# A hybrid decoder trunk: group A's level products by row halves, 16-blocks placed by ScalarE, attention scores in two-bank tiles

## The chip, the cores and the metric

The kernel runs on one core of one Trainium2 chip. The metric is the time of one execution on the device in microseconds; less is better. The time before is the median of three runs. The engines are called as the profile calls them: PE (TensorE's matmuls), PEld (its weight loads), DVE (VectorE), ACT (ScalarE), POOL (GpSimd) and SP (the queue that issues DMAs).

## The reference, cut to what matters

Two layers work on a stream of 1024 tokens by 1024 channels. Each layer has a token mixing part and a gated MLP, both between RMS norms. The mixing part projects the stream once, gives its columns to four groups of four heads, joins their outputs and projects them back. The change touches groups A, B and C.

Groups A (HGRN2, key width 64) and B (GLA, key width 32) are gated linear attention, `chunk_gla`: within a stretch of tokens, `attn[i,j] = sum_d q[i,d] k[j,d] exp(b[i,d] - b[j,d])` for `j <= i`, where `b` is the running sum of the log decays; across stretches a state is carried. Group C is causal softmax attention over blocks of 128 queries:

```
sc = (einsum('bqhd,bkhd->bhqk', qn, k_nope) + einsum('bqhd,bkd->bhqk', qr, k_rope)) * scale
p = softmax(where(mask, sc, -1e30))
o = einsum('bhqk,bkhv->bqhv', p, v)
```

Group D (a gated delta rule) and the MLP are not touched.

## The kernel before, in words

A layer runs: projections and group D (pools `p1`, `h`, `w`), then the **mixing stage** in which groups A, B and C are computed together, then the output projection, then the MLP. The mixing stage is the one that the change is in. It fills two stretches of the profiled execution, about 460 to 690 us in layer 0 and about 1943 to 2168 us in layer 1.

In the mixing stage `mixing` (L1068 ff.) drives two generators by turns, step for step, 32 steps of each (`NN`): `group_c` (attention, four heads of eight query blocks) and `ab` (groups A and B). `ab` runs three tiles of `gla_levels`: group B (HP = 4 heads of 32 rows on the 128 partitions), then the two halves of group A (HP = 2 heads of 64 rows), each with seven levels. While the levels of a tile run, `gla_chunks` of the tile before it runs too, one 128-token chunk per step; after the last tile its chunks run alone. A scheduler of the framework fixes the order of each engine's instructions ahead of time, with the program's order as priority and with the tiles' buffers as limits; at run time every engine takes its instructions in that order.

**A level** (`gla_levels`, L440 ff.) with half-block size s = 64, 32, 16, 8, 4, 2, 1 covers, in every block of 2s tokens, the pairs with the query in the second half and the key in the first. DVE (L479), POOL (L480) and ACT (L481) make the decay factors E, POOL multiplies k into them (L483). The queries are spread by head: for group B, DVE makes `qm` (L490) and ACT masks it into `Qb` once per head (L497, the mask column `hm` as the scale). For group A, DVE makes `Qb` directly with one masked product per head, two of 128x512 per level (L499); a head's columns of `Qb` are zero outside its 64 rows. Then PE multiplies 128x128 of K with 128 columns of `Qb` per chunk of 128 tokens (L504), both heads of group A side by side, four chunks to a PSUM tile of one bank; two such tiles make a level of group A, four make one of group B. Every fp32 matmul stands in the trace as two records. The wanted blocks of each tile are then placed in the SBUF tile `at`, which was cleared to zero: for s >= 32 by ACT copies (L509), one for each block row, below that by one DVE copy under a mask for each tile (L511).

**A chunk** (`gla_chunks`, L534 ff.) takes three PSUM tiles: `po` (state product, then the products with `at`, then DVE's sum at L555), `pk` (a transpose that ACT copies, L560) and `pS` (the state's update, which DVE folds in head by head, L565).

**A row of attention blocks** (`scores`, L750 ff.): query block t has (t+1)*128 keys. For each 512 of them one PSUM tile of one bank takes the score product (and on the last the causal mask, a bf16 product); DVE takes its maximum (L764), and for t >= 4 joins the two maxima while it scales (L767, else L769); ACT writes the exponentials of each tile with their sum (L773, an ACTIVATE and a read of its accumulator each); for t >= 4 DVE adds the two sums (L776); DVE takes the reciprocal (L778). `apply` then transposes the weights and multiplies them with the values; it is called two rows later (`LA = 2`).

**PSUM** has eight banks, in this stage split by `PS2 = dict(cs=4, ct=2, pm=2)`: four one-bank score tiles, two for `ct` (attention's other products) and two for `pm`, which all levels and chunks of groups A and B use by turns.

Of the kernel before, what the change touches and what calls it, by code (L numbers as in the profile page):

```python
# [13 lines left out]
ALU = mybir.AluOpType  # L14
# [114 lines left out]
class Body:  # L129
# [310 lines left out]
    def gla_levels(self, HP, load, sc, values, T):  # L440
# [12 lines left out]
        at = [self.t("g", "at", NAT, [128, cpa, HP, 128]) for _ in range(HP)]  # L453
# [5 lines left out]
        for s in LEVELS:  # L459
# [27 lines left out]
            if HP == 4:  # L487
                qm = small([128, 512], "qm", 2)
                qv = qm.rearrange("p (n s) -> p n s", s=s)
                nc.vector.tensor_tensor(out=qv, in0=hf(q, 1), in1=hf(E, 1), op=ALU.mult)  # L490
            for g in range(8 // CB):
                if g * CB % cps == 0:
                    z = slice(g * CB // cps * n2, (g * CB // cps + 1) * n2)
                    Qb = slot([128, cps, HP, 64])
                    for h in range(HP):
                        if HP == 4:
                            nc.scalar.activation(out=Qb[:, :, h, :], in_=qv[:, z], func=AF.Copy, scale=hm[:, h:h + 1])  # L497
                        else:
                            nc.vector.scalar_tensor_tensor(out=Qb[:, :, h, :], in0=hf(q, 1)[:, z], scalar=hm[:, h:h + 1],  # L499
                                                           in1=hf(E, 1)[:, z], op0=ALU.mult, op1=ALU.mult)  # L500
                p = self.ps([128, CB, HP, 64])
                for c in range(CB):
                    cc = g * CB + c
                    self.mm(p[:, c], K[:, cc * 128:(cc + 1) * 128], Qb[:, cc % cps].rearrange("p h i -> p (h i)"))  # L504
                A = at[g * CB // cpa][:, (g * CB) % cpa:(g * CB) % cpa + CB]
                if s >= 32:
                    for n in range(nbc):
                        r = slice(2 * s * n, 2 * s * n + s)
                        nc.scalar.copy(out=A[r, :, :, 2 * s * n + s:2 * s * n + 2 * s], in_=p[r, :, :, n * s:n * s + s])  # L509
                else:  # L510
                    nc.vector.copy_predicated(  # L511
                        out=A.rearrange("p c h (n e s) -> p (c h) n e s", e=2, s=s)[:, :, :, 1, :],
                        mask=mk.rearrange("p (n s) -> p n s", s=s)[:, None, :, :].to_broadcast([128, CB * HP, nbc, s]),
                        data=p.rearrange("p c h (n s) -> p (c h) n s", s=s))
# [19 lines left out]
    def gla_chunks(self, HP, T, out, f0):  # L534
# [9 lines left out]
        for c in range(8):  # L544
# [5 lines left out]
            for h in range(HP):  # L550
                self.mm(po[:, h * 64:h * 64 + 64], T["at"][c // (8 // HP)][:, c % (8 // HP), h, :], vc[:, h * 64:h * 64 + 64],
# [157 lines left out]
    def group_c(self, l, ckv, wv, load, krd, out):  # L709
# [40 lines left out]
        def scores(h, t):  # L750
# [3 lines left out]
            ps = []  # L754
            nm = small([128, 2], "nm", 4)
            for a in range(0, nk, 512):
                e = min(nk, a + 512)
                dg = e == nk
                p = self.ps([128, 512], "cs")[:, 0:e - a]
                self.mm(p, qc, K[:, a:e], True, not dg)  # L760
                if dg:
                    self.mm(p[:, e - a - 128:e - a], id16, caus, False, True)
                i = len(ps)
                nc.vector.tensor_reduce(out=nm[:, i:i + 1], in_=p, axis=AX.X, op=ALU.max)  # L764
                ps.append(p)
            if len(ps) == 2:
                nc.vector.tensor_scalar(out=nm[:, 0:1], in0=nm[:, 0:1], scalar1=nm[:, 1:2], scalar2=-scale, op0=ALU.max, op1=ALU.mult)  # L767
            else:
                nc.vector.tensor_scalar(out=nm[:, 0:1], in0=nm[:, 0:1], scalar1=-scale, scalar2=None, op0=ALU.mult)  # L769
            P = small(None, "P", LA + 1)  # L770
            sm = small([128, 2], "sm", 4)
# [898 lines left out]
```

## Time and profile before

| | us |
|---|---|
| runs before | 2966.41, 2962.98, 2966.25 |
| median | 2966.25 |
| the profiled execution's own time | 2966.38 |
| its span, first to last instruction | 2964.6 |
| busy in it: PE | 2743.4 (93%) |
| busy in it: DVE | 1881.0 (63%) |
| busy in it: ACT | 1272.3 (43%) |
| busy in it: POOL | 1192.4 (40%) |

The shares are means over stages with different limits. Matmuls are pipelined and their modelled ends overlap, so a PE that shows as busy need not be at its peak. A row of a group of instructions gives its count, the union of its busy time, the mean duration of one in ns, and the idle time of the engine ahead of them with what ended it.

### The profile page before, as it was taken

To read this page: it belongs to the slowest core of one execution; us is meant where nothing else is said; L and a number is where in the kernel's file an instruction comes from. 1 tells how busy PE (TensorE), PEld (TensorE's weight loads), DVE (VectorE), ACT (ScalarE), POOL (GpSimd) and SP (SyncE) were. 2 spreads that over 40 slices of the span, in tenths; PEclk is the share of its full clock that TensorE was granted. 3 is DMA by queue.
4 is the path that set the end of the run, shared out by engine and by line. 5 is a ranking of instruction groups with operands and counts; after the bars stand their busy time and mean duration, and the time that the engine had idled before them with its cause. 6 is when DMAs were issued, how large, how long until landed. Compare 5 with 4: busy or idle time off the path is not lost. (4 is left out here: it accounts for less than half of the span.)

```text
span 2964.6 us, 40009 instructions
## 1 busy us (share of the span) xinstructions
PE 2743.4 (93%) x14928; PEld 2223.9 (75%) x14928; DVE 1881.0 (63%) x2740; ACT 1272.3 (43%) x2338; POOL 1192.4 (40%) x1008
## 2 busy tenths in 40 slices
PE   7999898899869999999979998988998699999998
PEld 6787695677758888888767876856777588888887
DVE  5564426883697777764645645268836977777645
ACT  4523337555443333354434233375554433333443
POOL 2122654445765444300231327544457644443001
PEclk9999899999989999999989999999999899999999
DMA  3222653114423322376522226431143232223765
GB/s 122 70 83 69 238 185 122 60 45 135 136 68 100 100 98 99 121 261 187 174 70 69 84 76 236 178 122 62 43 135 135 68 103 96 99 100 103 258 197 192
DMA packets 152307, 362.94 MB, mean 122 GB/s; under 512 B 24337, under 2 KB 35889, under 8 KB 152113
## 3 DMA queue, kind: packets, MB, share of 16 engines
q1 hardware_dynamic: 152112, 360.39, 36.7%
q8 instruction: 117, 1.92, 0.3%
q14 instruction: 78, 0.63, 0.1%
HBM read 259.08 MB, written 101.25 MB: 122 GB/s over the span
## 5 line engine op out<-in xcount | busy, mean ns | idle before, releaser
L209 PE MATMUL pd<-h,wr 128*128 128x512 f32 x2624 | 664.8, 404 | 14.9 <-ACT wr L197 8.9
L198 POOL TENSOR_TENSOR wr<-wst,wr 128x512 fp32r<-128x512 f32 (+1 forms) x176 | 336.1, 1912 | 772.7 <-ACT wr L197 771.4
L209 PEld LDWEIGHTS pd<-h,wr 128*128 128x128 f32 x2624 | 493.9, 191 | 134.9 <-issue 11.4
L197 ACT CAST wr<-wst 128x512 fp32r<-128x512 f32 (+1 forms) x260 | 196.9, 759 | 373.0 <-PE pd L209 251.4
L209 PE MATMUL pd<-wr,h 128*128 128x256 f32 x1920 | 248.1, 290 | 1.1 <-issue 1.1
L209 PE MATMUL pm<-h,wr 128*128 128x512 f32 x848 | 235.2, 401 | 11.8 <-DVE x L1375 11.7
L209 PEld LDWEIGHTS pd<-wr,h 128*128 128x128 f32 x1920 | 240.8, 198 | 2.8 <-issue 1.4
L198 DVE TENSOR_TENSOR h<-st,h 128x1024 fp32r<-128x1024 f32 x120 | 152.6, 1273 | 122.6 <-ACT h L197 119.8
L209 PEld LDWEIGHTS pm<-h,wr 128*128 128x128 f32 x848 | 162.0, 191 | 52.2 <-DVE x L1375 12.5
L209 PE MATMUL pd<-wr,f 128*128 128x512 f32 x768 | 186.1, 399 | 11.4 <-POOL wr L198 10.5
L197 ACT CAST h<-st 128x1024 fp32r<-128x1024 f32 x120 | 125.6, 1048 | 146.4 <-PE pd L209 82.8
L209 PE MATMUL pd<-h 128*128 128x512 f32 x816 | 185.6, 389 | 0.0
L209 PEld LDWEIGHTS pd<-wr,f 128*128 128x128 f32 x768 | 143.6, 189 | 45.4 <-POOL wr L198 12.2
L209 PEld LDWEIGHTS pd<-h 128*128 128x128 f32 x816 | 153.2, 188 | 31.8
L209 PE MATMUL pm<-h 128*128 128x512 f32 x720 | 165.6, 390 | 0.8 <-DVE h L198 0.8
L1311 DVE SCALAR_TENSOR_TENSOR g<-z,pp,g 128x512 f32<-128x512 f32 x176 | 152.7, 868 | 7.3
L209 PEld LDWEIGHTS pm<-h 128*128 128x128 f32 x720 | 134.8, 188 | 29.6 <-DVE h L198 1.6
L1434 POOL TENSOR_TENSOR y<-y,gb 128x512 f32<-128x512 f32 x24 | 38.6, 1616 | 272.9 <-ACT fc L230 137.0
L215 PE MATMUL pm<-g,g 128*128 128x128 f32 (+1 forms) x672 | 118.3, 323 | 30.0 <-issue 12.9
L215 PEld LDWEIGHTS pm<-g,g 128*128 128x128 f32 x672 | 96.9, 198 | 57.4 <-issue 29.9
L1379 ACT COPY x<-pm 128x512 f32<-128x512 f32 x120 | 70.2, 585 | 152.8 <-PE pm L209 152.8
L209 PE MATMUL pm<-hs,wr 128*128 128x512 f32 x528 | 130.0, 394 | 3.2 <-POOL wr L198 3.2
(366 smaller groups left out, 5465.8 us busy)
## 6 DMA issues: line engine op xcount, KB each, us to landing
st<-gd SPq DMA_DIRECT2D x144, 256.0 KB, 3.0
wst<-in_wgu_dram SPq DMA_DIRECT2D x44, 512.0 KB, 3.6
ust<-in_wgu_dram SPq DMA_DIRECT2D x44, 512.0 KB, 3.6
gd<-g SPq DMA_DIRECT2D x88, 256.0 KB, 2.0
d<-in_wdn_dram SPq DMA_DIRECT2D x40, 512.0 KB, 5.5
td<-d SPq DMA_DIRECT2D x40, 512.0 KB, 3.1
st<-td SPq DMA_DIRECT2D x80, 256.0 KB, 3.6
st<-in_wdn_dram SPq DMA_DIRECT2D x68, 256.0 KB, 3.8
```

What stands on the lines that cost most here:

```text
L197: self.marks["hi"] = self.nc.scalar.copy(out=hi, in_=src)
L198: (eng or self.nc.gpsimd).tensor_tensor(out=lo, in0=src, in1=hi.bitcast(F32), op=ALU.subtract)
L209: mm = lambda x, y, **k: self.nc.tensor.matmul(out, lhsT=x, rhs=y, skip_group_check=onto, **k)
L215: self.nc.tensor.matmul(out, lhsT=lhsT, rhs=rhs, start=start, stop=stop)
L1311: nc.vector.scalar_tensor_tensor(out=c, in0=x[:, j:j + 512], scalar=w(j), in1=c, op0=ALU.mult, op1=ALU.add)
L1379: nc.scalar.copy(out=x, in_=p)
L1434: (dve if last and n else pool).tensor_tensor(out=y[t][:, c], in0=y[t][:, c], in1=g_post[:, c], op=ALU.mult)
```

## The change

It has three parts.

1. **Group A's level products by row halves.** For HP = 2 the masked queries `Qb` go. One DVE product per level makes `qm` from all 128 rows, with the constant scale `qscale` in place of the mask column. PE multiplies, per chunk and head, the head's 64 rows of K (64 rows by 128 columns as weights) with the head's 64 rows and 64 columns of `qm`: 16 matmuls of 64x64 operands in place of 8 of 128x128. Each head has a PSUM tile of its own (one bank) for all eight chunks, so both are filled side by side, and the placing follows after all 16. `at` is kept per head, [128, 8, 128]. Group B keeps its products.
2. **16-blocks are placed by ScalarE.** The limit between ACT's copies and DVE's masked copy moves from s >= 32 to s >= 16, for groups A and B: at s = 16 each tile is placed by four ACT copies of 16 partitions x 128 elements.
3. **A row of attention shares a two-bank tile.** The score tile becomes [128, 1024] in place of [128, 512], two of them in place of four (`cs=2`). All score products of a row go into it; then come one maximum over all keys, one scaling, one ACTIVATE with one read of the accumulator, one reciprocal. The join of the maxima and the sum of the two sums go.

```diff
@@ -450,7 +450,9 @@
         q, k, b = (load(j, slot()) for j in range(3))
         W = HP * 64
         CB, cpa, cps = 512 // W, 8 // HP, 1024 // W
-        at = [self.t("g", "at", NAT, [128, cpa, HP, 128]) for _ in range(HP)]
+
+        two = HP == 2
+        at = [self.t("g", "at", NAT, [128, 8, 128] if two else [128, cpa, HP, 128]) for _ in range(HP)]
         for x in at:
             nc.gpsimd.memset(x, 0.0)
         Qst, Kst = slot(), slot()
@@ -484,34 +486,46 @@
             mk = self.cm[:, LEVELS.index(s) * 64:(LEVELS.index(s) + 1) * 64]
             nbc = 64 // s
             n2 = cps * 64 // s
-            if HP == 4:
-                qm = small([128, 512], "qm", 2)
-                qv = qm.rearrange("p (n s) -> p n s", s=s)
+            qm = small([128, 512], "qm", 2)
+            qv = qm.rearrange("p (n s) -> p n s", s=s)
+            if two:
+                nc.vector.scalar_tensor_tensor(out=qv, in0=hf(q, 1), scalar=qscale, in1=hf(E, 1), op0=ALU.mult, op1=ALU.mult)
+            else:
                 nc.vector.tensor_tensor(out=qv, in0=hf(q, 1), in1=hf(E, 1), op=ALU.mult)
-            for g in range(8 // CB):
-                if g * CB % cps == 0:
-                    z = slice(g * CB // cps * n2, (g * CB // cps + 1) * n2)
-                    Qb = slot([128, cps, HP, 64])
-                    for h in range(HP):
-                        if HP == 4:
-                            nc.scalar.activation(out=Qb[:, :, h, :], in_=qv[:, z], func=AF.Copy, scale=hm[:, h:h + 1])
-                        else:
-                            nc.vector.scalar_tensor_tensor(out=Qb[:, :, h, :], in0=hf(q, 1)[:, z], scalar=hm[:, h:h + 1],
-                                                           in1=hf(E, 1)[:, z], op0=ALU.mult, op1=ALU.mult)
-                p = self.ps([128, CB, HP, 64])
-                for c in range(CB):
-                    cc = g * CB + c
-                    self.mm(p[:, c], K[:, cc * 128:(cc + 1) * 128], Qb[:, cc % cps].rearrange("p h i -> p (h i)"))
-                A = at[g * CB // cpa][:, (g * CB) % cpa:(g * CB) % cpa + CB]
-                if s >= 32:
+
+            def place(A, p):
+
+                if s >= 16:
                     for n in range(nbc):
                         r = slice(2 * s * n, 2 * s * n + s)
-                        nc.scalar.copy(out=A[r, :, :, 2 * s * n + s:2 * s * n + 2 * s], in_=p[r, :, :, n * s:n * s + s])
+                        nc.scalar.copy(out=A[r, :, 2 * s * n + s:2 * s * n + 2 * s], in_=p[r, :, n * s:n * s + s])
                 else:
                     nc.vector.copy_predicated(
-                        out=A.rearrange("p c h (n e s) -> p (c h) n e s", e=2, s=s)[:, :, :, 1, :],
-                        mask=mk.rearrange("p (n s) -> p n s", s=s)[:, None, :, :].to_broadcast([128, CB * HP, nbc, s]),
-                        data=p.rearrange("p c h (n s) -> p (c h) n s", s=s))
+                        out=A.rearrange("p c (n e s) -> p c n e s", e=2, s=s)[:, :, :, 1, :],
+                        mask=mk.rearrange("p (n s) -> p n s", s=s)[:, None, :, :].to_broadcast([128, 8, nbc, s]),
+                        data=p.rearrange("p c (n s) -> p c n s", s=s))
+
+            if two:
+                ps = [self.ps([128, 8, 64]) for _ in range(2)]
+                for c in range(8):
+                    for h in range(2):
+                        r = slice(64 * h, 64 * h + 64)
+                        self.mm(ps[h][:, c, :], K[r, c * 128:(c + 1) * 128], qm[r, c * 64:(c + 1) * 64])
+                for h in range(2):
+                    place(at[h], ps[h])
+            else:
+                for g in range(8 // CB):
+                    if g * CB % cps == 0:
+                        z = slice(g * CB // cps * n2, (g * CB // cps + 1) * n2)
+                        Qb = slot([128, cps, HP, 64])
+                        for h in range(HP):
+                            nc.scalar.activation(out=Qb[:, :, h, :], in_=qv[:, z], func=AF.Copy, scale=hm[:, h:h + 1])
+                    p = self.ps([128, CB, HP, 64])
+                    for c in range(CB):
+                        cc = g * CB + c
+                        self.mm(p[:, c], K[:, cc * 128:(cc + 1) * 128], Qb[:, cc % cps].rearrange("p h i -> p (h i)"))
+                    A = at[g * CB // cpa][:, (g * CB) % cpa:(g * CB) % cpa + CB]
+                    place(A.rearrange("p c h t -> p (c h) t"), p.rearrange("p c h t -> p (c h) t"))
             if s == 64:
 
                 bc = [128, 8, 64]
@@ -548,7 +562,8 @@
             if c:
                 self.mm(po, T["Q"][:, cl], St, True, False)
             for h in range(HP):
-                self.mm(po[:, h * 64:h * 64 + 64], T["at"][c // (8 // HP)][:, c % (8 // HP), h, :], vc[:, h * 64:h * 64 + 64],
+                a = T["at"][h][:, c, :] if HP == 2 else T["at"][c // 2][:, c % 2, h, :]
+                self.mm(po[:, h * 64:h * 64 + 64], a, vc[:, h * 64:h * 64 + 64],
                         c == 0, c == 0 or h == HP - 1)
             dv = small([128, W], "dv", 2)
             nc.gpsimd.tensor_tensor(out=hv(dv), in0=hv(vc), in1=T["dots"][:, c, :, None].to_broadcast([128, HP, 64]), op=ALU.mult)
@@ -751,31 +766,22 @@
             Q, K = QK[h]
             nk = (t + 1) * 128
             qc = Q[:, t * 128:(t + 1) * 128]
-            ps = []
-            nm = small([128, 2], "nm", 4)
+
+            p = self.ps([128, 1024], "cs")
+            nm = small([128, 1], "nm", 4)
             for a in range(0, nk, 512):
                 e = min(nk, a + 512)
                 dg = e == nk
-                p = self.ps([128, 512], "cs")[:, 0:e - a]
-                self.mm(p, qc, K[:, a:e], True, not dg)
+                self.mm(p[:, a:e], qc, K[:, a:e], True, not dg)
                 if dg:
-                    self.mm(p[:, e - a - 128:e - a], id16, caus, False, True)
-                i = len(ps)
-                nc.vector.tensor_reduce(out=nm[:, i:i + 1], in_=p, axis=AX.X, op=ALU.max)
-                ps.append(p)
-            if len(ps) == 2:
-                nc.vector.tensor_scalar(out=nm[:, 0:1], in0=nm[:, 0:1], scalar1=nm[:, 1:2], scalar2=-scale, op0=ALU.max, op1=ALU.mult)
-            else:
-                nc.vector.tensor_scalar(out=nm[:, 0:1], in0=nm[:, 0:1], scalar1=-scale, scalar2=None, op0=ALU.mult)
+                    self.mm(p[:, e - 128:e], id16, caus, False, True)
+            nc.vector.tensor_reduce(out=nm, in_=p[:, 0:nk], axis=AX.X, op=ALU.max)
+            nc.vector.tensor_scalar(out=nm, in0=nm, scalar1=-scale, scalar2=None, op0=ALU.mult)
             P = small(None, "P", LA + 1)
-            sm = small([128, 2], "sm", 4)
-            for i, p in enumerate(ps):
-                nc.scalar.activation(out=P[:, i * 512:i * 512 + p.shape[1]], in_=p, func=AF.Exp, scale=scale, bias=nm[:, 0:1],
-                                     accum_out=sm[:, i:i + 1])
-            if len(ps) == 2:
-                nc.vector.tensor_tensor(out=sm[:, 0:1], in0=sm[:, 0:1], in1=sm[:, 1:2], op=ALU.add)
+            sm = small([128, 1], "sm", 4)
+            nc.scalar.activation(out=P[:, 0:nk], in_=p[:, 0:nk], func=AF.Exp, scale=scale, bias=nm, accum_out=sm)
             rc = small([128, 1], "rc", 4)
-            nc.vector.reciprocal(out=rc, in_=sm[:, 0:1])
+            nc.vector.reciprocal(out=rc, in_=sm)
             return P, rc
 
         def apply(h, t, P, rc):
@@ -1638,7 +1644,7 @@
 NP, NU, NUL, NFIN = 10, 4, 4, 6
 
 LA = 2
-PS2 = dict(cs=4, ct=2, pm=2)
+PS2 = dict(cs=2, ct=2, pm=2)
 NN = (32, 32)
 
 HALF = (slice(0, 2), slice(2, 4))
```

## Rows read from the trace of the kernel before

**Rows 1.** Busy time by stretch, layer 0's mixing stage; columns in the first line.

```profile
core 0: us, PE busy (x) PEld busy (x) DVE busy (x) ACT busy (x) POOL busy (x), PEclk, DMA share, GB/s
460.00:680.00 220.00, 197.66 (x1187) 150.90 (x1185) 183.32 (x385) 130.79 (x337) 90.85 (x82) 0.97 0.18 59
...
480.00:520.00 40.00, 31.36 (x156) 23.25 (x157) 29.75 (x56) 34.02 (x86) 19.65 (x15) 1.00 0.20 60
500.00:560.00 60.00, 49.68 (x269) 34.89 (x267) 55.19 (x104) 39.06 (x101) 24.93 (x21) 1.00 0.21 66
580.00:640.00 60.00, 56.51 (x371) 45.75 (x369) 55.39 (x118) 31.89 (x81) 30.50 (x26) 0.94 0.21 65
```

**Rows 2.** Chain that ended last, layer 1's mixing stage (1943 to 2168 us), shares by line.

```profile
by line: PE pm L215 23.1%; PE ct L215 13.5%; PE cs L215 8.5%; DVE g L499 7.2%; DVE at L511 5.9%; issue 5.3%; PE ct L219 5.1%; ACT g L497 3.2%; DMA K<-kr 2.5%; DVE S L565 2.4%; DVE nm L764 1.9%; ACT g L481 1.9%; DVE qm L490 1.7%; DMA g<-Av 1
```

**Rows 3.** Groups by shape, 455 to 690 us: count, busy us, mean ns, idle before.

```profile
L511 DVE COPY_PREDICATED at<-cm,pm 128x512 f32<-128x512 int32 x40 | 37.1, 955 | 5.6 <-PE pm L215 5.0
L499 DVE SCALAR_TENSOR_TENSOR g<-g,cf,g 128x512 f32<-128x512 f32 x28 | 32.1, 1165 | 1.4 <-ACT g L481 1.4
...
L773 ACT ACTIVATE P<-cs,nm 128x512 f32<-128x512 f32 x24 | 16.5, 687 | 4.4 <-DVE nm L767 3.8 <-DVE nm L769 0.5
L764 DVE TENSOR_REDUCE nm<-cs 128x1 f32<-128x512 f32 x24 | 16.3, 681 | 1.3 <-PE cs L215 1.2
...
L773 ACT ACTIVATION_READ_ACCUMULATOR P<-cs,nm 128x1 f32 x48 | 9.6, 200 | 0.0
...
L509 ACT COPY at<-pm 32x256 f32<-32x256 f32 x16 | 5.8, 362 | 5.6 <-PE pm L215 5.4
L776 DVE TENSOR_TENSOR sm<-sm 128x1 f32<-128x1 f32 x16 | 5.7, 358 | 2.0 <-ACT P L773 1.9
...
L560 ACT COPY kT<-pm 128x128 f32<-128x128 f32 x21 | 5.5, 263 | 11.3 <-PE pm L219 11.2
...
L773 ACT ACTIVATE P<-cs,nm 128x128 f32<-128x128 f32 x8 | 2.9, 363 | 3.6 <-DVE nm L769 3.6
...
L764 DVE TENSOR_REDUCE nm<-cs 128x1 f32<-128x128 f32 x8 | 2.3, 286 | 1.2 <-PE cs L215 1.1
```

**Rows 4.** The same groups, ACT alone.

```profile
L529 ACT COPY dots<-pm 128x16 f32<-128x16 f32 x2 | 0.3, 172 | 4.6 <-PE pm L215 4.6
```

**Rows 5.** Timeline: a level of group A's first half; start us, us, engine.

```profile
592.14 1.78 DVE L499 SCALAR_TENSOR_TENSOR g<-g,cf,g 128x512 f32<-128x512 f32 x2
...
594.38 1.95 PE L215 MATMUL pm<-g,g 128*128 128x128 f32 x16
...
595.32 0.68 DVE L764 TENSOR_REDUCE nm<-cs 128x1 f32<-128x512 f32 x1
...
595.92 2.43 DVE L511 COPY_PREDICATED at<-cm,pm 128x512 f32<-128x512 int32 x2
```

**Rows 6.** Timeline of PE: levels of group A's second half.

```profile
637.99 1.06 PE L215 MATMUL pm<-g,g 128*128 128x128 f32 x8
...
639.10 1.06 PE L215 MATMUL pm<-g,g 128*128 128x128 f32 x8
639.99 0.41 PE L215 MATMUL pm<-S,g 128*128 128x128 f32 x2
...
643.20 1.06 PE L215 MATMUL pm<-g,g 128*128 128x128 f32 x8
```

**Rows 7.** Timeline of PE in group D: 64-row products (64*128) and their neighbours.

```profile
208.10 0.71 PE L215 MATMUL pm<-vn,kl 128*128 128x128 f32 x4
208.75 1.71 PE L215 MATMUL pm<-d,d 64*128 64x128 f32 x16
...
138.30 0.72 PE L215 MATMUL pm<-d,d 64*128 64x128 f32 x8
```

**Rows 8.** Busy time by stretch around a fall of the clock, columns as in rows 1.

```profile
555.00:561.00 6.00, 4.86 (x38) 4.32 (x39) 5.92 (x14) 2.15 (x8) 3.66 (x4) 1.00 0.01 3
562.00:568.00 6.00, 6.00 (x23) 5.25 (x24) 2.44 (x8) 2.02 (x4) 2.51 (x3) 0.50 0.00 1
```

## The prediction

> **What bounds the kernel now.** I read the stretches first, then the chain, then the groups, then timelines of single levels. All three edits lie in the mixing stage, about 225 us in each of two layers, 450 of 2966 us; the reader needs no other stage. In layer 0's 220 us PE shows 197.7 us busy and DVE 183.3, ACT 130.8 [rows 1]. No engine is full all the time. DVE is full from 500 to 560 us (55.2 of 60) and from 580 to 640 (55.4 of 60), but in the second of these PE shows 56.5 of 60 as well. Between 480 and 520 us, where group B's levels run, it is ACT that is nearly full: 34.0 of 40. The chain of layer 1's stage says the same [rows 2]: PE's `pm`, `ct` and `cs` lines hold 23.1 + 13.5 + 8.5 + 5.1 = 50%, DVE's named lines 7.2 + 5.9 + 2.4 + 1.9 + 1.7 = 19%. So DVE's work is worth its chain share at most, and PE stands close behind. I take both layers as alike.
>
> **Part 1, the masked products.** Two DVE products of 1.165 us per level become one: 14 of 28 go in a layer, 16.3 us of DVE work [rows 3]. Their line holds 7.2% of 225 us of chain = 16.2 us [rows 2], so half of them is worth **-8.1 us** a layer.
>
> PE: a level's product is 16 records in 1.95 us now [rows 5], and 8 take 1.06 [rows 6]: (1.06 - 0.275) / 7 = 0.112 us apart, the last one's tail being some 0.275 (an estimate from 16 records: 1.95 - 15 x 0.112). After the change it is 32 records of 64 rows. Group D already has such records: 8 of them took 0.72 us [rows 7]. One after another they would take 7 x 0.112 + 0.275 = 1.06; in four pairs 3 x 0.112 + 0.275 = 0.61. So upper and lower halves run side by side, and 32 records need about the 16 places of before. What is left over, 0.72 - 0.61 = 0.11 us, is a slow first record. Entering this mode shows too: four full-height records from 208.10 leave room for the next at 208.55, and the 64-row ones begin at 208.75 [rows 7], 0.1 us beyond one spacing. Leaving it I take as equal. That is 0.3 us more per level, 14 levels, 4.2 us; half of it on the chain, as PE holds half: **+2.1 us**. Bounds per level: no gain below 0.1, and 1.8 if nothing overlaps.
>
> Placing: until now a level's first tile was placed while PE filled the second. Now both heads' tiles fill together, so the first placing starts about one half product later, 1.06 us [rows 6], and both `pm` banks are held meanwhile. Behind them queue the chunk's `po`, then `pk` and `pS`, and DVE's update. In group A's first half DVE is late anyway: at 594.38 PE started, its first half was done by about 595.4, but DVE was at a maximum (595.32, 0.68 us) and placed from about 595.9 on [rows 5]. There I count nothing. In the second half's last five levels, about 5.2 us from one (637.99) to the next (643.20) with the chunk's products 0.9 us behind the second half product's start [rows 6], the wait is open: 5 x 0.95 = **+4.8 us** (the half run less the 0.1 by which it is usually late). Bounds: 0 to 14 x 1.06 = 14.8.
>
> **Part 2, the 16-blocks.** One of five masked levels leaves DVE: 8 of 40 copies of 0.955 us, 7.6 us of work [rows 3]; of the chain's 5.9% = 13.3 us a fifth, **-2.7 us**. ACT gets 32 copies of 16 partitions x 128 elements, which no row shows. The nearest are 128 elements at 0.263 us and, on the two sides, 256 elements at 0.362 [rows 3] and 16 elements at 0.172 [rows 4]. I take 0.263, the same element count: 8.4 us a layer, 5.5 to 11.6. Half of it falls on group B, where ACT is 85% busy [rows 1], and displaces masked queries and exponentials; I count a quarter of that half, **+1.0 us**. Group A's half lies beside free ACT time (31.9 of 60 busy from 580 to 640); with that cover gone it would cost up to 4.2.
>
> **Part 3, attention.** Sixteen rows a layer have t >= 4. A maximum costs 0.154 us plus 1.03 ns an element (0.681 at 512, 0.286 at 128), an exponential 0.255 plus 0.84 ns (0.687 and 0.363), a read of the sum 0.200 [rows 3]. Joining two tiles saves one fixed part each, and the 0.358 us addition: DVE 16 x (0.154 + 0.358) = 8.2 us, ACT 16 x (0.255 + 0.200) = 7.3 us. DVE's lines hold a fifth of the chain, so **-1.6 us**; ACT's I put against part 2's copies. Against it: two score tiles in place of four, so row t's products wait for the exponentials of row t - 2. Thirty-two rows in 225 us come 7 us apart, and the maximum starts only after all products, a bank's product later; the two-row lead covers both. Cost 0; if the cover goes, about 1 us in each of 16 rows.
>
> **The sum** per layer: -8.1 + 2.1 + 4.8 - 2.7 + 1.0 - 1.6 = -4.5, for both -9.0. The profiled execution took 2966.38 us (span 2964.6), 0.1 above the median, so the forecast is **2957 us**; its own range is 2945 to 2960.
>
> **The rivals.** *More gain*: DVE is the bound throughout its full stretches. 16.3 + 7.6 + 8.2 = 32.1 us of work leave DVE in each layer; 120 of the 220 us are full, 17.5 us, less 4 of PE's cost, for two layers 27: 2939. For it: just before the clock fell to 0.50 (the 1.2 GHz level) at 562, DVE was busy 5.9 of 6 us and PE 4.9 [rows 8]; six us at half clock cost three, and a fuller PE could spare them. Against it: PE at 56.5 of 60. Chance 0.12.
>
> *No change*: PE takes the place as soon as DVE is lighter, what DVE gave goes back in changes of mode and later placings: 2966. For it: half the chain is PE's. Chance 0.24.
>
> *Slower by the pair of banks*: each level must have both `pm` banks at once and gives neither back before its last product. Then all 28 levels pay 1.06 us, 29.7 in all, plus 4.2 for PE, against the relief of 8.1 + 2.7 - 1.0 + 1.6 = 11.4 a layer, 22.8: +11, **2977**. It decides from (22.8 - 4.2) / 1.06 = 18 levels of 28 on. For it: the levels of rows 6 take the two banks one after the other, 1.1 us apart, each as it comes free. Against it: late DVE hides it in the first half, and DVE will be less late at the updates too. Chance 0.17.
>
> *Slower by the halves in turn*: 32 records a level one after another, 1.5 us a level over my 0.3, 42 us of PE, half on the chain: 2978. Against it stand the 0.72 us of rows 7; for it the other row there, 16 records in 1.71 us, not far below the 15 x 0.112 + 0.275 = 1.96 of one after another. The order chosen ahead of time could come out so here. Chance 0.07.
>
> The Trainium skill (TensorE: Matmul & The Clock Gate, LDWEIGHTS (loading the stationary operand)) has a rule that leads there: a load costs by its columns, whatever its rows, so twice as many loads would take twice the time, and by that alone the sum is this rival's 2978. The same page (Part 3) lets loads of different row groups overlap; the 0.72 us of rows 7 agree with that, and the sum stays at the forecast.
>
> **How the numbers follow.** The forecast has 0.40, the rivals 0.12, 0.24, 0.17, 0.07. About 0.2%, 6 us, is what a measurement can tell. Faster: 0.40 + 0.12 = 0.52; the same 0.24; slower 0.17 + 0.07 = 0.24. The range reaches to the larger gain and beyond both slower cases, as the placing's bound alone spans 30 us: 2930 to 2980.
>
> **What would show it.** The masked product line at 14 a layer instead of 28; group A's products as 64-row records, a level's 32 within 2.1 us (3.6 would show the last rival); 16-partition copies near 0.26 us; maxima and exponentials of 640 to 1024 elements at 0.154 us + 1.03 ns and 0.255 us + 0.84 ns an element; DVE near 151 of 220 us; the stage shorter by 4 to 5 us in each layer. A longer wait of PE or ACT for `pm` in all levels of group A would show the pair of banks; a stage unchanged with DVE lighter, PE as the bound. Wrong altogether would be a difference outside the two mixing stages, or an ACT that holds group B back by more than the 4 us its copies take.

## The result and the profile after

The changed kernel takes **3063.2 us** (median of 4 runs, 3052.2 to 3079.6), the kernel before 2966.3 beside it: ratio **1.0327 [1.0301, 1.0352]**, 97 us slower. Forecast were 2957 us and at most 2980. The profiled execution took 3079.6 us, the longest of the four. The page, busy time and granted clock (each digit a fortieth of the span, in tenths):

```profile
span 3077.9 us, 40827 instructions
...
PE 2863.1 (93%) x15376; PEld 2324.7 (76%) x15376; DVE 1829.4 (59%) x2632; ACT 1281.7 (42%) x2338; POOL 1189.8 (39%) x1008
...
PEclk9999899679989999999989999996899899999999
```

DVE has 108 instructions and 52 us less, where 64 us of work were meant to go. PE is busy 120 us more. The clock is low in the slices of the two mixing stages and hardly elsewhere. From the last product of L209 ahead of a stage to the first one behind it, layer 0 takes 297.8 us in place of 242.1 and layer 1 293.3 in place of 241.6: 107 of the 113 us by which the span grew. In layer 0's stage PE is busy for 270.8 us (214.5 before) and idle for 27.0 (27.6): all that was added is busy PE. By stretches of layer 0 (columns as in [rows 1]):

```profile
core 0: us, PE busy (x) PEld busy (x) DVE busy (x) ACT busy (x) POOL busy (x), PEclk, DMA share, GB/s
460.00:730.00 270.00, 245.97 (x1337) 190.03 (x1338) 154.89 (x314) 128.79 (x323) 94.80 (x85) 0.82 0.16 54
480.00:520.00 40.00, 31.95 (x138) 24.06 (x136) 21.23 (x38) 35.65 (x90) 17.04 (x12) 0.87 0.13 38
560.00:580.00 20.00, 20.00 (x89) 15.06 (x89) 9.35 (x17) 8.16 (x22) 6.54 (x7) 0.67 0.01 2
580.00:600.00 20.00, 20.00 (x79) 16.88 (x79) 5.52 (x13) 3.01 (x7) 6.38 (x6) 0.50 0.08 26
600.00:620.00 20.00, 20.00 (x100) 16.66 (x99) 9.70 (x22) 4.74 (x11) 4.87 (x5) 0.66 0.17 53
620.00:640.00 20.00, 20.00 (x111) 17.46 (x109) 11.52 (x27) 6.13 (x16) 2.28 (x3) 0.74 0.28 93
```

Where DVE was full and the clock at 0.94 [rows 1], PE is now busy without a gap, at a clock of 0.50 to 0.74, and DVE works 5.5 to 11.5 of 20 us. So DVE was relieved and PE became the bound, at half its speed for some of the time. Twice the length times (1 - granted clock) gives the time at half clock (1.2 GHz): 96 us of layer 0's stage and 85 of layer 1's, against 14 and 10 before. The chain of layer 1 says the same; PE's `pm` line holds 38.3% (23.1% in [rows 2]), DVE's placing 2.7% and its masked products 1.4%:

```profile
by line: PE pm L215 38.3%; PE ct L215 18.2%; PE cs L215 9.1%; issue 7.4%; PE ct L219 4.9%; DVE g L481 3.4%; DVE at L503 2.7%; DVE qm L492 1.4%; PE pm L219 1.4%; ACT g L522 1.4%; POOL g L485 1.3%; DVE g L533 1.2%; DVE g L535 1.0%; ACT PT L79
```

The groups that answer to [rows 3], layer 0's stage (line, engine, shapes, count, busy us, mean ns, idle before):

```profile
L215 PE MATMUL pm<-qm,g 64*128 64x64 f32 x448 | 59.6, 324 | 5.9 <-POOL g L478 2.5 <-DVE rc L784 1.9 <-DVE nm L779 1.5
...
L503 DVE COPY_PREDICATED at<-cm,pm 128x512 f32<-128x512 int32 x32 | 31.5, 1013 | 37.9 <-PE pm L215 37.6
...
L492 DVE SCALAR_TENSOR_TENSOR qm<-g,g 128x512 f32<-128x512 f32 x14 | 11.8, 843 | 7.7 <-PE pm L215 6.3 <-ACT g L471 1.3
...
L501 ACT COPY at<-pm 16x128 f32<-16x128 f32 x32 | 8.2, 256 | 8.2 <-PE pm L215 7.8
...
L778 DVE TENSOR_REDUCE nm<-cs 128x1 f32<-128x1024 f32 x3 | 3.7, 1221 | 1.3 <-PE cs L215 1.3
...
L782 ACT ACTIVATE P<-cs,nm 128x1024 f32<-128x1024 f32 x3 | 3.3, 1106 | 0.0
```

Counts are as forecast, 14 products among them, and so are these durations: 16-partition copies of 256 ns (263 were taken), a maximum of 1024 elements in 1.221 us (1.21 by the two terms), an exponential in 1.106 (1.12). A product takes 0.843 us where 1.165 was taken. New is DVE's idle time for PE ahead of the placing: 37.6 us, where [rows 3] has 5.0. Four levels of group A show why:

```profile
start us, us, engine line op out<-in xcount [idle before <-releaser]
545.95 2.00 PE L215 MATMUL pm<-qm,g 64*128 64x64 f32 x32 [0.93 <-POOL g L478]
...
570.05 2.00 PE L215 MATMUL pm<-qm,g 64*128 64x64 f32 x16
...
572.08 1.06 ACT L501 COPY at<-pm 16x128 f32<-16x128 f32 x4 [0.91 <-PE pm L215]
...
573.03 2.00 PE L215 MATMUL pm<-qm,g 64*128 64x64 f32 x16
...
585.88 3.67 PE L215 MATMUL pm<-qm,g 64*128 64x64 f32 x16
...
592.02 3.67 PE L215 MATMUL pm<-qm,g 64*128 64x64 f32 x16
...
694.63 2.94 PE L215 MATMUL pm<-qm,g 64*128 64x64 f32 x32
```

The first level alternates its halves: 32 records in 2.00 us. The level from 570.05 runs head 0's 16 records, 2.00 us by themselves, and head 1's from 573.03. The one from 585.88 does the same at half clock, 3.67 us a half. By the order of PE's instructions, 10 of 14 levels in a layer run six or more products (two records each) of one half before the other half. Seven of them run all eight, then other products, then the other half, as the second and third here: 4.0 us at the full clock. The other three, the last line among them, overlap where the half changes and take 2.94 to 3.17 us. Why the order is so was not measured by itself; it fits that each half's products are given to PE as their own `pm` bank comes free, since the halves alternate in the two kernels below that give both banks at one time.

### The profile page after: what moved, and what is told of

Read it like the earlier page. It is cut to its first block, busy times and chain, and to the rows that moved or that the text cites. A ratio compares the mean times of both kernels' runs of the same rounds, so it can differ in the third digit from the quotient of the medians.

```text
span 3077.9 us, 40827 instructions
## 1 busy us (share of the span) xinstructions
PE 2863.1 (93%) x15376; PEld 2324.7 (76%) x15376; DVE 1829.4 (59%) x2632; ACT 1281.7 (42%) x2338; POOL 1189.8 (39%) x1008
## 5 line engine op out<-in xcount | busy, mean ns | idle before, releaser
L209 PE MATMUL pd<-h,wr 128*128 128x512 f32 x2624 | 666.0, 404 | 15.9 <-ACT wr L197 8.9
L209 PEld LDWEIGHTS pd<-h,wr 128*128 128x128 f32 x2624 | 494.9, 191 | 135.9 <-ACT wr L197 11.6
L209 PE MATMUL pd<-wr,h 128*128 128x256 f32 x1920 | 246.9, 290 | 0.0
L209 PE MATMUL pm<-h,wr 128*128 128x512 f32 x848 | 235.5, 401 | 11.8 <-DVE x L1381 11.8
L209 PEld LDWEIGHTS pd<-wr,h 128*128 128x128 f32 x1920 | 239.8, 197 | 1.8 <-issue 0.4
L209 PEld LDWEIGHTS pm<-h,wr 128*128 128x128 f32 x848 | 162.2, 192 | 51.6 <-DVE x L1381 12.7
L209 PE MATMUL pd<-wr,f 128*128 128x512 f32 x768 | 190.3, 405 | 11.5 <-POOL wr L198 10.0
L209 PE MATMUL pd<-h 128*128 128x512 f32 x816 | 185.6, 389 | 0.0
L209 PEld LDWEIGHTS pd<-wr,f 128*128 128x128 f32 x768 | 146.6, 194 | 46.9 <-POOL wr L198 11.8
L209 PEld LDWEIGHTS pd<-h 128*128 128x128 f32 x816 | 153.2, 188 | 31.8
L209 PE MATMUL pm<-h 128*128 128x512 f32 x720 | 167.1, 393 | 0.0
L209 PEld LDWEIGHTS pm<-h 128*128 128x128 f32 x720 | 136.6, 190 | 28.5
L215 PEld LDWEIGHTS pm<-qm,g 64*128 64x128 f32 x896 | 110.0, 230 | 31.1 <-issue 16.9
L209 PE MATMUL pm<-hs,wr 128*128 128x512 f32 x528 | 130.6, 395 | 2.6 <-POOL wr L198 2.6
L209 PE MATMUL pd<-hs,wr 128*128 128x512 f32 x528 | 129.2, 393 | 0.0
```

The lines of the kernel that those rows point to most:

```text
L209: mm = lambda x, y, **k: self.nc.tensor.matmul(out, lhsT=x, rhs=y, skip_group_check=onto, **k)
L215: self.nc.tensor.matmul(out, lhsT=lhsT, rhs=rhs, start=start, stop=stop)
```

## Experiments

Each run is also told as a share of the 2966 us by its ratio. full and pm4 were timed once and have no interval. Stretches of layer 0's mixing stage stand in the table, as worked out from the timeline: *B* from the stage's start to DVE's first sum of a chunk of group B (group B's levels), *A1* from there to the first sum of group A's first half (its levels beside B's chunks), *A2* to the first sum of its second half, *rest* the last chunks and what is left of attention, and us at half clock in the whole stage, from its granted clock. Each row is of one execution: in bench (below), whose stages are those of the kernel before, instruction for instruction, the two stages have 3 and 17 us at half clock where the kernel before has 14 and 10, so ten us in that column say little.

| kernel | median us | ratio [95%] | B | A1 | A2 | rest | half clock |
|---|---|---|---|---|---|---|---|
| before | 2966 to 2970 | 1 | 95.8 | 67.5 | 45.0 | 33.8 | 14 |
| changed | 3063.2 | 1.0327 [1.0301, 1.0352] | 100.3 | 95.6 | 63.2 | 38.6 | 96 |
| p1 | 3049.0 | 1.0259 [1.0229, 1.0289] | 99.3 | 82.4 | 54.6 | 40.7 | 61 |
| p23 | 2995.4 | 1.0080 [1.0065, 1.0096] | 101.1 | 66.6 | 51.1 | 36.5 | 27 |
| full | 3039.4 | timed once | 100.1 | 73.1 | 65.4 | 39.5 | 44 |
| pm4 | 3032.1 | timed once | 108.6 | 61.7 | 59.4 | 45.2 | 61 |
| wide | 3023.9 | 1.0183 [1.0168, 1.0199] | 105.8 | 72.1 | 52.8 | 38.6 | 34 |
| paircs | 3023.0 | 1.0176 [1.0163, 1.0189] | 90.2 | 80.1 | 57.3 | 38.9 | 61 |
| p2 | 2987.6 | 1.0054 [1.0041, 1.0068] | 98.3 | 63.6 | 46.8 | 38.3 | 10 |
| p3 | 2986.7 | 1.0054 [1.0042, 1.0066] | 96.5 | 66.8 | 52.7 | 35.3 | 21 |
| p2a | 2992.3 | 1.0078 [1.0063, 1.0094] | 97.7 | 64.4 | 50.1 | 41.4 | 27 |
| p3b | 3008.8 | 1.0132 [1.0114, 1.0149] | 98.8 | 70.6 | 50.0 | 40.7 | 27 |
| act0 | 2969.3 | 1.0001 [0.9989, 1.0013] | 95.9 | 60.1 | 44.5 | 42.4 | 21 |
| act0_n34 | 2963.1 | 0.9987 [0.9976, 0.9997] | 96.2 | 60.1 | 47.3 | 36.3 | 12 |

**Which part costs.** p1 is the changed kernel with parts 2 and 3 taken back, p23 with part 1 taken back.

> Part 1 alone, the row halves; parts 2 and 3 as in the kernel before. Common to every theory that puts the loss on part 1: 3050 to 3090 us, the clock at half for over 70 us in each mixing stage. If the loss were due to the two-bank score tiles or to ACT's placing: 2955 to 2975, since the halves alone would then be the small gain that was forecast.

> Parts 2 and 3 alone, group A's queries masked on DVE as before, full-height products. If part 1 is the whole loss: 2945 to 2970 us, by the forecast's own terms (2 x (-2.7 + 1.0 - 1.6) = -6.6) near 2960, and no more than about 15 us at half clock in a mixing stage, as before. If the pair of score banks or the 16-row copies carry a part of the loss: above 2980.

p1 is 77 us slower, p23 24: together 101, beside 97 for all three parts. Part 1 has most of the loss, a little less than expected (3049 us for 3050 or more, 61 and 58 us at half clock for over 70). Of the 35 us by which layer 0's stage grew, 25 are in the levels of group A. p23 came out by its second case: parts 2 and 3 lose by themselves where the forecast had 6.6 us of gain.

**Height, columns, order.** Four kernels take part 1 apart. full undoes only the height:

```diff
-  r = slice(64 * h, 64 * h + 64)
-  self.mm(ps[h][:, c, :], K[r, c * 128:(c + 1) * 128], qm[r, c * 64:(c + 1) * 64])
+  self.mm(ps[h][:, c, :], K[:, c * 128:(c + 1) * 128], qh[h][:, c * 64:(c + 1) * 64])
```

> The changed kernel, its records of group A's level products made of full height again: queries masked per head on DVE, all 128 rows of K as weights, and the same 16 products of 64 columns into the same two pm banks. So the number of records, the banks and the waits for them stay as changed; only the height differs. Theory clock (half-height records let the granted clock fall): the half-clock time falls from some 90 us a mixing stage to under 30, and although 32 records now run one after another (3.6 us a level) and DVE has its 14 products back, the time is under 3030 us, near 3000. Theory turn (the loss is the records one after another, 1.5 us a level, and the low clock only follows from DVE waiting for PE): 3050 us or more, the clock at half as long as in the changed kernel.

Between the two: 3039.4, the clock at half for 44 and 34 us. Against p23, with the same work on DVE, 32 records of 64 columns in place of 16 of 128 cost 44 us; 28 levels by 1.65 (3.6 - 1.95 [rows 5]) are 46. That is near, but not the same thing by itself: full has 24 us more at half clock than p23, worth up to 12, and takes its banks otherwise. Against the changed kernel it is 24 us *faster* although DVE has 14 products a layer more to do, with 79 us at half clock in the two stages in place of 181.

pm4 sets `PS2 = dict(cs=1, ct=2, pm=4)`; paircs takes a level's two halves as one tile:

```diff
-  ps = [self.ps([128, 8, 64]) for _ in range(2)]
+  pp = self.ps([128, 2, 8, 64], "cs")
+  ps = [pp[:, h] for h in range(2)]
```

> The changed kernel with four pm banks in place of two, paid for by one two-bank score tile in place of two. The order chosen ahead then has the two halves alternating in nearly every level. Theory turn: a level of group A takes 2.0 to 2.2 us of PE at full clock instead of 3.6, the clock stays as before (under 20 us at half in a stage), 2960 to 2990 us. Theory clock: the halves run side by side but are half-height records all the same, the clock is at half for over 60 us in a stage, 3020 us or more. Its one score tile could cost by itself up to 1 us in each of 64 rows of attention blocks, 64 us in all, which would show as DVE and PE idle in attention at full clock.

> The changed kernel, a level's two halves in one tile of two banks, which it takes from the score tiles: one wait for both banks, so the order chosen ahead alternates the halves. The pm banks are left to group B and the chunks. Theory turn (pairs side by side take a level back to 2.0 to 2.2 us of PE, the clock follows): under 50 us at half clock in a stage, 2980 to 3020 us with the cost of parts 2 and 3 still in it. Theory height: still over 70 us at half clock, 3040 us or more. Attention and the levels now share two tiles, which could cost by itself up to 1 us in each of 28 levels.

In both the halves alternate, and a level takes what was forecast at full clock; two levels of paircs in the timeline (start us, us):

```profile
548.37 3.68 PE L215 MATMUL cs<-qm,g 64*128 64x64 f32 x32 [0.26 <-POOL g L478]
...
579.84 2.00 PE L215 MATMUL cs<-qm,g 64*128 64x64 f32 x32
```

That takes back 31 and 40 us, but not the rest: the clock is at half for some 60 us a stage, where theory turn had under 20 and under 50. pm4 came out close to theory clock (over 60 us, 3020 or more); paircs fits neither of its theories. pm4, with one score tile, also has 8 us more in B than the changed kernel and 7 more in the rest. At half clock the same 32 records take 3.68 us. The trace shows what stands ahead of the longest fall in paircs:

```profile
543.60:547.60 4.00, 3.20 (x24) 2.69 (x23) 3.42 (x8) 3.11 (x6) 0.86 (x2) 1.00 0.00 0
547.60:578.30 30.70, 27.46 (x154) 22.54 (x153) 19.44 (x28) 11.60 (x31) 19.84 (x14) 0.50 0.06 18
```

The clock falls at 547.6 us, ahead of the stage's first half-height record (548.37) and behind a stretch with gaps in PE, so these records did not start that fall. Of the seven falls in the changed kernel's layer 0, two come behind 4 us in which PE had no gap (at 576.1, the longest, and 627.3), the other five behind 4 us in which it was busy for 1.1 to 3.6. What starts a fall, and why the clock falls as often in pm4 and paircs, is not shown.

wide keeps the half height and moves 128 columns:

```diff
-  self.mm(ps[h][:, c, :], K[r, c * 128:(c + 1) * 128], qm[r, c * 64:(c + 1) * 64])
+  e = min(c * 64 + 128, 512)
+  self.mm(ps[h].rearrange("p c i -> p (c i)")[:, c * 64:e], K[r, c * 128:(c + 1) * 128], qm[r, c * 64:e])
```

> The changed kernel, where each half-height record of group A's level products moves 128 columns in place of 64: its own 64 and the next chunk's, which the next product of the same head overwrites (the last chunk of a head keeps 64). Order, banks, weights, waits and results stay; only the columns that PE moves per record double. In turn, records are 0.112 us apart with 64 columns or 128, so at full clock the products take no longer. Theory columns (the clock falls because records of 64 columns in turn leave PE without columns to move for half of its busy time): more columns make the kernel faster, half-clock time from some 90 us a mixing stage to under 50, 3005 to 3045 us. Theory height (rows that stand idle let the clock fall): the clock is at half as long as in the changed kernel, 3055 us or more.

Nearly twice the columns, and 39 us faster, with 34 and 38 us at half clock. That speaks for theory columns, but the order moved too: only 4 levels of a layer, not 10, run six or more products of one half in turn. So bench measures the disputed thing by itself:

```diff
+  up, lo, al = slice(0, 64), slice(64, 128), slice(0, 128)
+  one = lambda p, r, c, n: self.mm(p[:, 0:n], K[r, c * 128:c * 128 + 128], q[r, c * 64:c * 64 + n])
+  turn = lambda ru, rl, n: [(p, r, c, n) for p, r in ((a, ru), (b, rl)) for c in range(8)]
+  for seq in (turn(al, al, 64), turn(up, lo, 64), [x for c in range(8) for x in ((a, up, c, 64), (b, lo, c, 64))],
+              turn(up, lo, 128), turn(al, al, 128)):
+      for _ in range(16):
+          for x in seq: one(*x)
+      apart()
```

> The kernel before with streams of products behind its end, on PE alone with nothing to wait for, from two loaded tiles; their results are dropped. Five blocks of 512 records, between blocks 96 records of full height and 512 columns (some 40 us): (1) full height, 64 columns, 16 records into one bank, then 16 into the other; (2) the same with the upper half's 16 and then the lower half's 16; (3) halves alternating, 64 columns; (4) as (2) with 128 columns; (5) as (1) with 128 columns. Theory columns: (1) and (2) alike fall to half clock and take some 110 us each, (3) to (5) stay at full clock with some 30, 57 and 57 us. Theory height: (1) and (5) at full clock, (2) and (4) at half. Theory gaps (the clock falls only where PE waits, so not in a stream without waits): all five at full clock, 57, 57, 30, 57, 57 us.

Stretches of bench inside block (1), the products between, (2), those between, (3), (4) and (5):

```profile
core 0: us, PE busy (x) PEld busy (x) DVE busy (x) ACT busy (x) POOL busy (x), PEclk, DMA share, GB/s
3020.00:3070.00 50.00, 50.00 (x450) 50.00 (x449) 0.00 (x0) 0.00 (x0) 0.00 (x0) 1.00 0.00 1
3072.00:3112.00 40.00, 40.00 (x94) 17.67 (x93) 0.00 (x0) 0.00 (x0) 0.00 (x0) 1.00 0.00 0
3120.00:3190.00 70.00, 70.00 (x430) 70.00 (x430) 0.00 (x0) 0.00 (x0) 0.00 (x0) 0.50 0.00 1
3200.00:3236.00 36.00, 36.00 (x85) 15.96 (x84) 0.00 (x0) 0.00 (x0) 0.00 (x0) 1.00 0.00 0
3238.00:3266.00 28.00, 28.00 (x508) 28.00 (x504) 0.00 (x0) 0.00 (x0) 0.00 (x0) 1.00 0.01 2
3310.00:3354.00 44.00, 44.00 (x487) 44.00 (x487) 0.00 (x0) 0.00 (x0) 0.00 (x0) 1.00 0.01 1
3398.00:3452.00 54.00, 54.00 (x486) 54.00 (x485) 0.00 (x0) 0.00 (x0) 0.00 (x0) 1.00 0.00 1
```

From their first to their last record the blocks take 57.0, **81.7**, 28.5, 46.6 and 57.1 us. All three theories miss. Full height with 64 columns keeps the clock, half height with 128 columns too, and so do half-height pairs; only half height *and* 64 columns *in turn* runs at half clock, with PE busy for 70.00 of 70 us and waiting for nothing. The products behind it have the full clock again. Each block ran once, in this one order. That is the form which part 1 gave to 10 levels of 14, and the stretch at 580 us above shows it in the kernel, among other products; the three levels that overlap in part ran at the full clock. Within one half the records of blocks (2) and (4) come 0.213 and 0.112 us apart, but at each change of the half some of them overlap. So block (4) takes less than (5), and (2) less than twice (1).

**Why parts 2 and 3 lose.** p2 and p3 are each part alone; p3b takes two-bank tiles but leaves maxima, exponentials and sums apart; p2a leaves group B's 16-blocks with DVE.

```diff
 p3b:  + pp = self.ps([128, 1024], "cs")
       - p = self.ps([128, 512], "cs")[:, 0:e - a]
       + p = pp[:, a:e]
 p2a:  - if s >= 16:
       + if s >= (16 if HP == 2 else 32):
```

> Part 3 alone: a row's scores in one two-bank tile, two of them in place of four single banks. Theory banks (a row waits for the exponential of the second row before it, so attention cannot run between group B's levels): 2980 to 2995, and a stretch of some 20 us in group B's levels without score products. Theory ACT: 2955 to 2968.

> The kernel before with a row's score banks taken as one tile of two banks, two such tiles in place of four single banks; maxima, exponentials and sums stay apart, one for each bank. So it is part 3's wait without its savings on DVE and ACT. Theory banks (the wait costs what part 3 costs): 2985 to 3000, the 17 us of part 3 alone and up to 8 us a stage for the savings that are missing. Theory joined (the long maximum and exponential of 1024 elements delay DVE and ACT): 2966 to 2975.

Theory banks holds: two tiles without the joining (p3b) cost 39 us, more than its range of 2985 to 3000 had, joining them gives back 23, and part 3 is left with 16. The place was wrong: it is A2 that grows, by 7.7 us in p3, not group B's levels. The weights of the score products, p3 and then before: idle time ahead of them for an exponential grew from 1.7 to 6.1 us in layer 0. These 4.4 us are part of the 9.2 by which p3's stage is longer there; in p3b that wait is 4.8 us, and the stage 18 us longer. The rest was not traced to a wait.

```profile
L215 PEld LDWEIGHTS cs<-K,Q 128*128 128x128 f32 x96 | 15.2, 194 | 10.0 <-ACT P L784 6.1 <-DVE Q L764 2.2 <-issue 1.4
```

```profile
L215 PEld LDWEIGHTS cs<-K,Q 128*128 128x128 f32 x96 | 15.0, 194 | 5.3 <-issue 1.8 <-ACT P L773 1.7 <-DVE Q L747 1.2
```

> Part 2 alone: ACT places the 16-blocks, the rest as before. Theory ACT (parts 2 and 3 together cost 27 us because ACT's 32 copies a layer of group B's half lie on a full ACT and hold its levels back): 2980 to 2995. Theory banks (the pair of score banks costs them): 2955 to 2968.

> Part 2 alone, for group A's levels alone; group B's 16-blocks stay with DVE. Theory B (ACT's copies cost in group B's levels, where ACT is nearly full): the 18 us of part 2 alone are gone, 2960 to 2970. Theory order (the cost lies in the two stretches behind and at the stage's end, where rows of attention are left over): 2978 or more.

p2 is 16 us slower, and p2a, without group B's half, 23: theory B falls. The table's layer 0 shows the smaller part of p2's loss: that stage is 4.9 us longer, layer 1's 12.3, with 34 us at half clock there (10 before). In p2, p2a and act0 (below) three rows of attention are left behind the last chunk, two before, and in p2a's A2 the clock falls beside the small sums of q times k (2 columns a record, 213 ns apart at half clock). Four runs tried these. `n34` merges the streams with `NN = (34, 32)`, `dw` moves 64 columns of the same constants in those sums:

> Part 2 alone (ACT places the 16-blocks of both groups) with the weight of 34 to 32. Theory leftover (most of part 2's 18 us is the same three rows at the end of the stage, 14 and 17 us in place of 10): 2965 to 2975. Theory ACT (its copies hold the levels back): 2980 or more, as without the weight.

> The control: the kernel before with the same weight of 34 to 32. One and a half rows are left behind its last chunk, so there is less to win. Theory leftover: 0 to 6 us faster a stage, 2955 to 2966. Theory moved: 2964 to 2972.

> ACT's placing of group A's 16-blocks alone, with the same 64 columns in place of 2 or 4. Its trace shows those 16 records by themselves, 0.213 us apart at half clock, where the kernel before has level products beside them. Theory narrow: the half-clock time of some 28 us a layer falls by 10 or more, 2975 to 2985 in place of 2992. Theory order (where work stands in the queues costs, the clock only follows): 2987 to 2995.

> The kernel before; its eight products a level of 16 that sum q times k by head (128 x 2 or 128 x 4 columns) move 64 columns of the same constants in place of 2 or 4; the copy reads the same columns. PE's time for such a record is set by its weights, 0.11 us at full clock, so the products take no longer. Theory narrow (records with hardly a column let the clock fall too; the kernel before shows its fall in group A's first half beside them): some 7 us less at half clock a layer, 2 to 4 us faster a layer, 2960 to 2966. Rival: the fall has other causes, 2966 to 2970.

p2_n34: 2984.9, 1.0065 [1.0046, 1.0084], above theory leftover. The last stretch (behind the last chunk) fell from 14.4 to 7.5 us, and A2 grew from 46.8 to 55.4, so the time moved.

before_n34: 2973.0, 1.0020 [1.0009, 1.0031], above both of its ranges.

p2a_dw: 2990.1, 1.0075 [1.0061, 1.0089]; A2's half clock is gone (10 to 0 us), its time fell by 2, the total by nothing that shows: theory order.

before_dw, which adds next to no work for PE (sixteen of those records take 1.84 us before, 1.89 to 1.95 now at the full clock), is 7 us *slower*, outside both of its ranges: 2974.7, 1.0023 [1.0013, 1.0032], with 16.6 us behind its last chunk in place of 10.1 and 38 us at half clock in layer 0; its profiled execution was the longest of ten. The order moved: in layer 0's stage 1064 of PE's 1273 instructions keep their order, told by the tiles that they write and read. So an edit that moves the order can cost about that by itself.

What makes up the rest of part 2's 16 us stays open.

**The relief of DVE without the halves.** act0 is the kernel before with group A's queries masked by ACT.

> The kernel before, group A's queries masked as group B's are: one product on DVE and two masked copies of 512 elements on ACT a level, in place of two masked products on DVE. PE's records stay as before. It is the relief of DVE that part 1 was made for, without its price on PE. If DVE's products are worth their share of the chain: 8 us less a stage and some 1 to 3 back for ACT, 2950 to 2960. If what waits next is one step longer (DVE, then ACT, then PE): 2966 to 2985.

> The masked queries of group A by ACT as in the run before it, and the streams merged with a weight of 34 to 32 in place of 32 to 32, so that the order chosen ahead puts all attention products ahead of the last chunk. Theory leftover (that kernel's 8 us shorter middle of a stage is lost at the end of it, where three rows of attention stand in PE's queue behind the last chunk's products, 19 us in place of 10): the end of the stage is 8 to 10 us shorter, 2950 to 2960 us. Theory moved (the same work stands somewhere, so what leaves the end comes back ahead of it): 2965 to 2972.

> The masked queries by ACT, the weight of 34 to 32 and the 64 columns together, the candidate against both kernels. In that kernel no clock falls beside those records, so theory narrow gives nothing more: 2958 to 2966, below the kernel before by 0.1 to 0.3%.

act0 shortens A1 by 7.4 us, and what is left of attention takes it back: 19.0 us behind the last chunk in place of 10.1. The time, 2969.3, is in the second of its two ranges. With `n34` that is 7.9, and the kernel is 4 us faster than the one before, 0.9987 [0.9976, 0.9997]; with `dw` too 2967.3 beside 2970.0, 0.9990 [0.9981, 0.9998]. Both are the fastest here, by less than the 6 us that count as a difference.

## Why the prediction was wrong

- **The failed step** is in part 1: "So upper and lower halves run side by side, and 32 records need about the 16 places of before." They can (32 records in 2.00 us; bench, 512 in 28.5), but PE takes them in its queue's order, and that order runs one half ahead of the other in 10 of 14 levels, so that at the full clock seven cost 4.0 us and three about 3.0 in place of 1.95. The rows for it were at hand. In [rows 7] the 8 records of 0.72 us start in pairs 13 ns apart; the 16 records of 1.71 us start 0.11 us apart, but for three pairs in the middle: there the halves come in turn, and overlap only where the half changes. The sum took the first of the two rows. What the two banks' waits do to the order was weighed in it only as a late placing.
- **A term was missing**: the clock. It stood in the forecast as something that a fuller PE could spare [rows 8]; that the new records themselves lower it was no case. At half clock for 181 us of the two stages against 24, PE loses up to half of the 157 more, 78 us. In layer 0 that is 41 of the 56 us by which PE is busier, and the levels in turn, 7 x 2.05 + 3 x 1.07 = 18 us, are about the rest (an estimate). full has 79 us at half clock with records of the same columns and full height, so the height of such records is worth about 100 of the 157; p23, without part 1, has 55.
- *Slower by the halves in turn* (0.07) had the right mechanism and 1.5 us a level: full against p23 gives 44 us, its 42, though up to 12 of the 44 may be the clock. It put only half of that on the chain, though PE then has no gap, and had no clock: 2978 in place of 3063. *The pair of banks* is not what is seen in 10 of 14 levels: there the halves do not wait for each other, which is the trouble.
- **DVE's relief** of part 1 came near where it lies: 8.1 us a layer forecast, 7.4 in A1 of act0, which relieves DVE in another way. That it stays did not hold: the end of the stage took it back.
- **Part 2** was to give 1.7 us a layer; it cost 8. Its copies are as forecast (8.2 us a layer), so the loss does not come from copies that are longer than forecast.
- **Part 3**: "two-row lead covers both. Cost 0" failed. Two tiles cost 39 us in the two layers (bound: 32). Joining was worth 23, not 3.
- **DVE's load** fell by less than named: 32 us were to leave each layer (183 to 151 in the 220 us of [rows 1]), and in layer 0's whole stage it is 191.3 us before and 170.1 after, 21 less. Eighteen products that the change did not touch (L481) took 21 us where they had taken 14.8; why is open.
- Right were the counts and the durations of ACT's copies, of the maxima and of the exponentials.

The Trainium skill (TensorE: Matmul & The Clock Gate, LDWEIGHTS (loading the stationary operand)) has a load cost by its columns, and by that alone the halves double a level's time. Where they come in turn, the trace agrees: 16 records take 2.00 us at 64 rows, 1.95 at 128 [rows 5]. Where they alternate, the overlap that Part 3 of that page of the Trainium skill describes is what the trace shows.

## What to carry to other kernels

Products of half height can pay only where the queue alternates the halves, and here not even there, as pm4 and paircs stayed 37 and 28 us slower than p23, which keeps the full height and has the same parts 2 and 3 (pm4 with one score tile less): look at the order of PE's records, not at whether two halves could overlap, and give both halves' banks at one time. Before narrowing products, ask what they leave of the granted clock: measure a stream of the new form by itself, which takes one run. Where an order is chosen ahead of time, run an edit that moves it and adds next to no work as a control; here it was worth 7 us, as much as the gains in question.

## What was not expected of the hardware

A PE that is never idle can run at half clock (1.2 GHz). In bench, half-height records of 64 columns in turn ran at 0.50 with PE at 70.00 of 70 us and PEld too, while the same count at full height, with 128 columns, or in alternating halves kept 1.00. The Trainium skill (TensorE: Matmul & The Clock Gate, Part 1) ties the clock to how busy PE is and its fall to idleness; block (2) differs, and the measurement decides. A record of half height is also no cheaper: within a run of one half it is 0.112 us apart, as at 128 rows, with 64 columns or 128.
